# The last two expert blocks' rows stay in SBUF and are added to their tokens by one-hot products

## The chip, the cores and the metric

The kernel runs on one core of one Trainium2 chip. The metric is the device time of one execution in microseconds (us). Engines are named as the profile names them: PE is TensorE (matrix products, PEld its weight loads), DVE is VectorE, ACT is ScalarE, POOL is GpSimd, SP is SyncE, which here only issues DMAs. A q behind a name (POOLq, SPq) is that engine's instruction queue.

## The reference

One decoder layer over 512 tokens of 1024 features. What matters here is its last part, a mixture of 64 experts with 8 experts per token, and the layer norm that ends the program:

```
def routed_experts(xf, idx, gate_w, w_gate, w_up, w_down):
    # sort the token-expert assignments by expert, one or more blocks of rows per expert
    ...
    def block_fn(args):
        toks, e = args
        xb = x_pad[toks]
        return swiglu(xb, w_gate[e], w_up[e], w_down[e])
    yb = lax.map(block_fn, (row_tok.reshape(n_blocks, MOE_BLOCK), block_e))
    y = yb.reshape(n_rows, d) * row_w[:, None]
    return jax.ops.segment_sum(y, row_tok, num_segments=n_tok + 1)[:n_tok]
...
        moe = swiglu(xf, w_sh_gate[l], w_sh_up[l], w_sh_down[l]) + \
            routed_experts(xf, idx, gate_w, ...)
        x = layer_norm(ALPHA * x + moe.reshape(bsz, seq, d), ln3_g[l], ln3_b[l])
    return x
```

Each token's output is ALPHA times its input, plus the shared expert, plus the weighted rows of its eight experts, normalised over the 1024 features.

## The kernel before

Before the experts come the input projections, the two mixers, cross-attention, routing and the shared expert. None of that is touched. The expert stage runs N = 65 blocks in the order of the list `queue`: one block of up to 128 token rows for each of the 64 experts, and one overflow block (the entry None) for an expert with more than 128 rows. Blocks are numbered here from 0 to 64.

Every fp32 operand of a product is split into a high and a low fp32r part: `split` (L80) casts the high part on ACT and subtracts it on DVE for the low part. `mm3` (L83 to L85) then runs three products for one. Iteration n of the loop does, in source order, the up and gate products of block n (`block_up`, tiles ehi, elo), the gated hidden rows of block n - 1 (`block_h`, tiles hh, hth, htl), the loads of the weights of block n + 1 (`load_gu`, on SP), the split of the down weights of block n - 1 (`down_split`, tiles dhi, dlo), the token rows of block n + 1 (`prepare_x`: transposes, tile xb, and a gather on POOL), and the down products of block n - 1 (`block_down`). Weights land in ten SBUF slots that the class `Ring` hands out in turn; each block takes three of them.

`block_down` copies its two 128x512 PSUM results to the tile ys on ACT (L754, L755). A DMA from POOL (L756) then scatters the 128 rows to their tokens and adds them to a sum in DRAM. There are two such sums, `accs[0]` and `accs[1]` (acc_79 and acc_80 below, `accv` a view of each in four chunks of 128 tokens). They start as ALPHA times the input and as the shared expert. Blocks alternate between them by `target(n)`: block 61 goes to sum 0, block 62 to sum 1, and the last two blocks, 63 and 64, both to sum 0. A scatter waits for the one before it on the same sum.

In the last iteration the four chunks X[0] to X[3] (tiles y, two chunks each) are loaded by SP from sum 1 (L945). After the last block comes a loop over further overflow blocks (`tc.For_i`, L953) whose count is read from a register. With these inputs its body runs no time, but where it ends every engine waits until all engines and all DMAs issued so far are done. Behind it POOL adds sum 0 to X by four accumulating DMAs (L969). Each chunk is then normalised: chunks 0 and 2 by `centred` on DVE, chunks 1 and 3 by `norm_in` on ACT. The reciprocal square root is a power on POOL (L120, L152), DVE applies gain and shift (L979), and ACT issues the write of the output (L980).

Instructions stand on their engines in an order that a scheduler makes at build time; it may move an instruction ahead of the source's order, but not past what it depends on.

Of the kernel before, what the change touches and what calls it, by code (L numbers as in the profile page):

```python
# [9 lines left out]
FT = mybir.dt.float32  # L10
FR = mybir.dt.float32r
# [3 lines left out]
OP = mybir.AluOpType  # L15
# [3 lines left out]
T = 512  # L19
D = 1024  # L20
KC = 8
NCH = 4
# [5 lines left out]
ALPHA = 2.0 ** 0.25  # L28
# [10 lines left out]
def decoder_layer(ctx: ExitStack, tc: tile.TileContext, I, out, dbg=None):  # L39
    nc = tc.nc  # L40
# [41 lines left out]
    def mm3(ps, s, m, start, stop):  # L82
        nc.tensor.matmul(ps, s[0], m[0], start=start, stop=False)  # L83
        nc.tensor.matmul(ps, s[0], m[1], start=False, stop=False)  # L84
        nc.tensor.matmul(ps, s[1], m[0], start=False, stop=stop)  # L85
# [26 lines left out]
    def centred(dst, src, g):  # L112
        st = sm.tile([128, 2, 6], FT, name="st", tag="st")
        for j in range(2):
            nc.vector.bn_stats(st[:, j], src[:, j * 512:(j + 1) * 512])
        mv = sm.tile([128, 2], FT, name="mv", tag="mv")
        nc.vector.bn_aggr(mv, st)
        rs = sm.tile([128, 1], FT, name="rs", tag="rs")
        nc.vector.tensor_scalar(rs, mv[:, 1:2], EPS, None, op0=OP.add)
        nc.gpsimd.tensor_tensor(rs, rs, mhalf, op=OP.pow)  # L120
        nc.vector.scalar_tensor_tensor(dst, src, mv[:, 0:1], g, op0=OP.subtract, op1=OP.mult)
        return rs
# [6 lines left out]
    xTl = xp.tile([128, KC, T], FR, name="xTl", tag="xTl")  # L129
    X = row_pair("X01", "x01") + row_pair("X23", "x23")  # L130

    def residual(c, n0, ps, sums):
        sl = X[c][:, n0:n0 + 512]
        nc.vector.scalar_tensor_tensor(sl, sl, ALPHA, ps, op0=OP.mult, op1=OP.add,
                                       accum_out=sums[:, c, n0 // 512:n0 // 512 + 1])

    def norm_in(c, gb, junk):
        nm = sm.tile([128, 1], FT, name="nm", tag="nm")
        nc.scalar.activation(junk, X[c], AF.Identity, accum_out=nm)
        nc.vector.tensor_scalar(nm, nm, -1.0 / D, None, op0=OP.mult)  # L140
        return norm_tail(c, nm, gb, junk)
# [239 lines left out]
    with tc.tile_pool(name="pm", bufs=1, reuse_waits="tile") as pm:  # L381
# [34 lines left out]
        for c in range(NCH):  # L416
            cs = slice(c * 128, (c + 1) * 128)
            ps = accps()
# [305 lines left out]
    def block_h(hp, gate):  # L724
        hh = late[0].tile([128, EH], FT, name="hh", tag="hh")
        nc.scalar.activation(hh, hp[:, 0:EH], AF.Silu)
        mark[0] = nc.vector.scalar_tensor_tensor(hh, hp[:, EH:2 * EH], gate, hh, op0=OP.mult, op1=OP.mult)
        hv = hh.rearrange("t (p k) -> t k p", k=2)
        hps = zps().rearrange("p (k t) -> p k t", k=4)
        for k in range(2):  # L730
            nc.tensor.transpose(hps[:, k], hv[:, k], idf)
        hth = late[0].tile([128, 2, 128], FR, name="hth", tag="hth")
        htl = late[0].tile([128, 2, 128], FR, name="htl", tag="htl")
        split(hth, htl, hps[:, 0:2])
        return hth, htl

    def down_split(wd):
        w = []
        for k in range(2):
            hi = wq.tile([128, D], FR, name="dhi", tag="h")  # L740
            lo = wq.tile([128, D], FR, name="dlo", tag="l")
            split(hi, lo, wd[:, k])
            w.append((hi, lo))
        return w

    def block_down(w, h, idx, acc):

        yps = [accps(), accps()]
        for k in range(2):
            for j in range(2):  # L750
                js = slice(j * 512, (j + 1) * 512)
                mm3(yps[j], (h[0][:, k], h[1][:, k]), (w[k][0][:, js], w[k][1][:, js]), k == 0, k == 1)
        ys = late[0].tile([128, D], FT, name="ys", tag="ys")
        nc.scalar.copy(ys[:, 0:512], yps[0])  # L754
        nc.scalar.copy(ys[:, 512:1024], yps[1])  # L755
        nc.gpsimd.indirect_dma_start(out=accs[acc], out_offset=bass.IndirectOffsetOnAxis(ap=idx, axis=0),  # L756
                                     in_=ys, in_offset=None, bounds_check=T - 1, oob_is_err=False,
                                     compute_op=OP.add)
# [151 lines left out]
        block_x(gx.pop(queue[n]), n % 2)  # L910
        fetch_next()

    def target(n):
        return (n + 1) % 2 if n < N - 2 else 0

    ovx = []
    vs = block_views(0)
# [3 lines left out]
    for n in range(N):  # L921
        if n == N - 6:
            ring.drop(XT)
        idx, gt = entry(queue[n])
        hp = accps()
        block_up(gu, n % 2, 0, hp)
        if prev:
            h = block_h(prev[1], prev[3])
        block_up(gu, n % 2, 1, hp)
        down_v = vs[2]  # L930
        if n + 1 < N:
            vs = block_views(n + 1)
            gu = load_gu(*vs[0:2])
        if prev:
            wd = down_split(prev[0])
        if n + 1 < N:
            prepare_x(n + 1)
        if prev:
            block_down(wd, h, prev[2], target(n - 1))
        prev = (load_d(down_v), hp, idx, gt)  # L940
        if n == N - 1:

            X[:] = row_pair("y01", "x01") + row_pair("y23", "x23")
            for c in range(NCH):
                nc.sync.dma_start(X[c], accv[1][:, c])  # L945
            fg, fb = row_pair("fin", "t01")
            junk = xx.tile([128, D], FT, name="junk", tag="t2")
            nc.scalar.dma_start(fg, bcast(I["ln3_g"], D))
            nc.scalar.dma_start(fb, bcast(I["ln3_b"], D))
    block_down(down_split(prev[0]), block_h(prev[1], prev[3]), prev[2], 0)  # L950

    nov = nc.values_load(novi[0:1, 0:1], min_val=1, max_val=32)
    with tc.For_i(1, nov, 1):  # L953
        eii, *ov = overflow_list(opl)
        overflow_entry(*ov)
        idx, gt = entry(None)
        xg = gather(idx)
        vs = overflow_views(eii)
        gu, wd = load_gu(*vs[0:2]), load_d(vs[2])
        block_x(xg, 0)  # L960
        hp = accps()
        block_up(gu, 0, 0, hp)
        block_up(gu, 0, 1, hp)
        block_down(down_split(wd), block_h(hp, gt), idx, 0)


    ov_ = out[0].rearrange("(c t) d -> t c d", t=128)
    for c in range(NCH):
        nc.gpsimd.dma_start(X[c], accv[0][:, c], accum_op=OP.add)  # L969
    for c in range(NCH):  # L970
        if c in (0, 2):
            rs = centred(X[c], X[c], fg)
        else:
            rs = norm_in(c, (fg, None), junk)
        parts = 2 if c == NCH - 1 else 1
        w = D // parts
        for i in range(parts):
            sl = slice(i * w, (i + 1) * w)
            nc.vector.scalar_tensor_tensor(X[c][:, sl], X[c][:, sl], rs, fb[:, sl], op0=OP.mult, op1=OP.add)  # L979
            nc.scalar.dma_start(ov_[:, c, sl], X[c][:, sl])  # L980


class Ring:
# [10 lines left out]
    def drop(self, tags):  # L994
        self.slots = [s for s in self.slots if s[1] not in tags]

    def tile(self, shape):
        pool, tag = self.slots.pop(0)
        self.slots.append((pool, tag))
        return pool.tile(shape, FT, name="wraw", tag=tag, bufs=1)  # L1000


_INS = ["x", "mem", "ln_in_g", "ln_in_b", "w_in", "b_in", "ln_v_g", "ln_v_b", "w_spatial", "b_spatial",
# [22 lines left out]
```

## Time and profile before

| what | us |
|---|---|
| median of 3 runs | 1244.97 (1244.26 to 1245.07) |
| the profiled execution's own time | 1245.57 |
| its span, from first to last instruction | 1243.9 |
| PE busy in the span | 1180.3 (95%) |
| scatter of block 62 issued | 1196.47 |
| last copy of the last block out of PSUM begins | 1208.08 |
| last scatter landed, all engines released from the loop's end | 1218.29 |
| last chunk of the sum landed in X | 1232.82 |

The profile is one execution. Its page gives busy time by engine, the span in 40 slices, DMA queues, the chain of work that ended last, and the costliest groups of instructions. The trace behind it can be asked for the same by window, engine and line. The profiled execution's time is 1.67 us over its span, and the median of the runs is 0.60 us below that execution's time, so the median is the span and 1.07 us.

### The profile page before, as it was taken

What the parts mean: (1) busy time and instruction counts of PE and PEld (TensorE: products, weight loads), DVE (VectorE), ACT (ScalarE), POOL (GpSimd) and SP (SyncE); (2) the same over time, 40 slices, a digit from 0 to 9 for tenths busy, and PEclk for the clock granted to TensorE, in tenths of its full rate; (3) what the DMA queues carried; (4) which work ended last, traced back from release to release, by engine and by line L of the source; (5) the groups of instructions that cost most, each with busy time, mean ns of one, the idle gap of its engine ahead of it and who ended that gap; (6) DMA issues with size and microseconds to landing.
All of it is one profiled execution on the core that took longest, in us unless ns stands there. A gap on an engine that the chain in (4) does not pass through costs nothing.

```text
span 1243.9 us, 17778 instructions
## 1 busy us (share of the span) xinstructions
PE 1180.3 (95%) x6301; PEld 996.3 (80%) x6301; DVE 976.0 (78%) x1512; ACT 805.4 (65%) x1198; POOL 281.3 (23%) x179
## 2 busy tenths in 40 slices
PE   7999999999999999999999999999999999899980
PEld 6887888878888889887888888888888888788860
DVE  6546556464754577886999999999999999999974
ACT  6443334342324346536898888989889899699961
POOL 2000000000200010220334433434334343234313
PEclk9999999999999999999999999999999999899995
DMA  9621322224333223478999999999999999799946
GB/s 338 212 83 58 106 68 68 68 68 153 124 115 131 78 83 120 160 253 317 346 394 367 376 404 359 374 377 395 381 378 393 346 385 395 264 373 342 384 110 149
DMA packets 102368, 307.74 MB, mean 247 GB/s; under 512 B 17358, under 2 KB 35334, under 8 KB 93446
## 3 DMA queue, kind: packets, MB, share of 16 engines
q1 hardware_dynamic: 78054, 259.05, 54.6%
q0 software_dynamic: 19296, 35.71, 12.2%
q10 hardware_dynamic: 4928, 11.83, 2.5%
q8 instruction: 50, 0.82, 0.3%
q14 instruction: 40, 0.33, 0.1%
HBM read 298.64 MB, written 42.47 MB: 274 GB/s over the span
## 4 chain that ended last, share of the span: by engine, by line
PE 69%; DVE 9%; DMA 9%; issue 8%; POOL 3%; ACT 2%; SPq 0%; POOLq 0%; DVEq 0%; ACTq 0%
PE acc L84 20%; PE acc L85 20%; PE acc L83 20%; PE trp L170 4%; DMA wraw<-in_w_exp_gate_dram 2%; DMA acc<-ys,idxs 2%; DVE qq L283 2%; POOL acc L756 2%; DMA wraw<-in_w_exp_up_dram 1%; DMA wraw<-in_w_exp_down_dram 1%; DVE elo L80 1%; DMA ln<-in_ln_in_g_dram 1%; PE zp L84 1%; POOL xg L686 1%; PE zp L83 1%
## 5 line engine op out<-in xcount | busy, mean ns | idle before, releaser
L80 DVE TENSOR_TENSOR elo<-wraw,ehi 128x1024 fp32r<-128x1024 f32 x260 | 313.6, 1224 | 15.4 <-ACT ehi L80 14.4
L80 ACT CAST ehi<-wraw 128x1024 fp32r<-128x1024 f32 x260 | 274.3, 1056 | 45.5 <-PE acc L85 42.4
L84 PE MATMUL acc<-elo,xb 128*128 128x512 f32 x520 | 206.5, 397 | 5.1 <-DVE elo L80 3.9
L83 PE MATMUL acc<-ehi,xb 128*128 128x512 f32 x520 | 209.4, 403 | 1.2 <-ACT xb L80 1.2
L85 PE MATMUL acc<-ehi,xb 128*128 128x512 f32 x520 | 206.0, 396 | 1.1 <-DVE xb L80 1.1
L756 POOL DMA_INDIRECT acc<-ys,idxs x65 | 148.4, 2283 | 213.8 <-ACT ys L755 199.4
L80 DVE TENSOR_TENSOR wlo<-wraw,whi 128x1024 fp32r<-128x1024 f32 x84 | 101.9, 1223 | 105.1 <-ACT whi L80 105.1
L80 ACT CAST whi<-wraw 128x1024 fp32r<-128x1024 f32 x84 | 87.5, 1051 | 127.6 <-PE acc L84 72.1
L84 PE MATMUL acc<-xTl,whi 128*128 128x512 f32 (+1 forms) x448 | 162.3, 363 | 0.0
L83 PE MATMUL acc<-xTh,whi 128*128 128x512 f32 (+1 forms) x448 | 162.0, 362 | 0.0
L85 PE MATMUL acc<-xTh,wlo 128*128 128x512 f32 (+1 forms) x448 | 160.7, 360 | 0.0
L80 DVE TENSOR_TENSOR dlo<-wraw,dhi 128x1024 fp32r<-128x1024 f32 x130 | 156.6, 1220 | 0.4 <-ACT dhi L80 0.2
L80 ACT CAST dhi<-wraw 128x1024 fp32r<-128x1024 f32 x130 | 137.5, 1057 | 29.5 <-PE acc L85 21.4
L686 POOL DMA_INDIRECT xg<-x2d,idxs x65 | 90.3, 1389 | 231.0 <-PE trp L170 172.8
L84 PEld LDWEIGHTS acc<-elo,xb 128*128 128x128 f32 x520 | 98.4, 189 | 24.4 <-DVE elo L80 4.4
L85 PEld LDWEIGHTS acc<-ehi,xb 128*128 128x128 f32 x520 | 98.2, 189 | 22.0 <-DVE xb L80 2.0
L83 PEld LDWEIGHTS acc<-ehi,xb 128*128 128x128 f32 x520 | 98.8, 190 | 20.4 <-ACT xb L80 1.4
L83 PE MATMUL acc<-dhi,hth 128*128 128x512 f32 x260 | 106.1, 410 | 0.5 <-ACT hth L80 0.5
L85 PE MATMUL acc<-dhi,htl 128*128 128x512 f32 x260 | 102.9, 396 | 0.0
L84 PE MATMUL acc<-dlo,hth 128*128 128x512 f32 x260 | 102.5, 394 | 0.0
L83 PEld LDWEIGHTS acc<-xTh,whi 128*128 128x128 f32 x448 | 84.5, 189 | 12.1
L84 PEld LDWEIGHTS acc<-xTl,whi 128*128 128x128 f32 x448 | 84.6, 189 | 11.6
(278 smaller groups left out, 2168.8 us busy)
## 6 DMA issues: line engine op xcount, KB each, us to landing
wraw<-in_w_exp_gate_dram SPq DMA_DIRECT2D x130, 512.0 KB
wraw<-in_w_exp_up_dram SPq DMA_DIRECT2D x130, 512.0 KB
wraw<-in_w_exp_down_dram SPq DMA_DIRECT2D x65, 1024.0 KB
wraw<-in_w_in_dram SPq DMA_DIRECT2D x28, 1024.0 KB
wraw<-in_w_mem_kv_dram SPq DMA_DIRECT2D x4, 1024.0 KB
wraw<-in_w_out_dram SPq DMA_DIRECT2D x4, 1024.0 KB
X<-in_x_dram SPq DMA_DIRECT2D x4, 512.0 KB
wraw<-in_w_mem_q_dram SPq DMA_DIRECT2D x2, 1024.0 KB
```

The lines of the kernel that those rows point to most:

```text
L80: return nc.scalar.copy(hi, src), nc.vector.tensor_sub(lo, src, hi.bitcast(FT))
L83: nc.tensor.matmul(ps, s[0], m[0], start=start, stop=False)
L84: nc.tensor.matmul(ps, s[0], m[1], start=False, stop=False)
L85: nc.tensor.matmul(ps, s[1], m[0], start=False, stop=stop)
L170: nc.tensor.transpose(ps[:, k], sv[:, k0 + k], idf)
L283: nc.vector.tensor_tensor_scan(qq[:, 0:n][:, ::-1], sy[:, 1:n + 1][:, ::-1], ones.to_broadcast([128, n]), 1.0, op0=OP.mult, op1=OP.mult)
L686: nc.gpsimd.indirect_dma_start(out=xg, out_offset=None, in_=x2d, in_offset=bass.IndirectOffsetOnAxis(ap=idx, axis=0), bounds_check=T - 1, ...
L756: nc.gpsimd.indirect_dma_start(out=accs[acc], out_offset=bass.IndirectOffsetOnAxis(ap=idx, axis=0), in_=ys, in_offset=None, bounds_check=T ...
```

## The change

Block 63 and block 64 are no longer scattered. `block_keep` leaves the 128 rows of a block in SBUF, split into a high and a low part, in two ring slots, and makes a one-hot matrix oh[row, token] from the block's token numbers against the constant row 0 to 511 (iotaT). Behind the loop `kept_rows` forms, for each chunk of 128 tokens and each half of the features, the product of the one-hot matrix with those rows: four products (two blocks, high and low) into one PSUM tile, 32 in all. `residual` (L134, with scale 1) adds them to X on DVE and sums each row on the way. All four chunks are then normalised by `residual_norm`, with ACT's squares. SP loads X from sum 0 as it stands after block 61, and POOL adds sum 1, as it stands after block 62, by the four accumulating DMAs, which now stand ahead of the loop's end. The loop's own body, which doesn't run here, adds its rows in the same way.

```
-    def residual(c, n0, ps, sums):
+    def residual(c, n0, ps, sums, scale=ALPHA):
...
+    def block_keep(yps, idx):
+        tok = sm.tile([128, 1], FT, name="tok", tag="nm")
+        nc.vector.tensor_copy(tok, idx)
+        if not ohs:
+            o = ring.tile([128, 4, T], FR)
+            ohs.extend(o[:, i] for i in range(4))
+        oh = ohs.pop(0)
+        y = ring.tile([128, 2, D], FR)
+        hi, lo = y[:, 0], y[:, 1]
+        nc.vector.tensor_scalar(oh, iotaT, tok, None, op0=OP.is_equal)
+        for j in range(2):
+            js = slice(j * 512, (j + 1) * 512)
+            split(hi[:, js], lo[:, js], yps[j])
+        return oh, hi, lo
+
+    def kept_rows(kept, c, n0):
+        ps = accps()
+        last = 2 * len(kept) - 1
+        i = 0
+        for oh, hi, lo in kept:
+            for y in (hi, lo):
+                nc.tensor.matmul(ps, oh[:, c * 128:(c + 1) * 128], y[:, n0:n0 + 512], start=i == 0, stop=i == last)
+                i += 1
+        return ps
...
-    def target(n):
-        return (n + 1) % 2 if n < N - 2 else 0
+    kept, ohs = [], []
+    iotaT = xx.tile([128, T], FT, name="iotaT", tag="t3")
+    nc.gpsimd.iota(iotaT, pattern=[[1, T]], base=0, channel_multiplier=0, ...)
...
-        if prev:
-            block_down(wd, h, prev[2], target(n - 1))
+        if n == N - 1:
+            kept.append(block_keep(down(wd, h), prev[2]))
+        elif prev:
+            block_down(wd, h, prev[2], n % 2)
...
-                nc.sync.dma_start(X[c], accv[1][:, c])
+                nc.sync.dma_start(X[c], accv[n % 2][:, c])
...
+            for c in range(NCH):
+                nc.gpsimd.dma_start(X[c], accv[(n - 1) % 2][:, c], accum_op=OP.add)
-    block_down(down_split(prev[0]), block_h(prev[1], prev[3]), prev[2], 0)
+    kept.append(block_keep(down(down_split(prev[0]), block_h(prev[1], prev[3])), prev[2]))
...
+    sums = sm.tile([128, NCH, 2], FT, name="fsums", tag="fsums", bufs=1)
     for c in range(NCH):
-        nc.gpsimd.dma_start(X[c], accv[0][:, c], accum_op=OP.add)
-    for c in range(NCH):
-        if c in (0, 2):
-            rs = centred(X[c], X[c], fg)
-        else:
-            rs = norm_in(c, (fg, None), junk)
+        for n0 in (0, 512):
+            residual(c, n0, kept_rows(kept, c, n0), sums, 1.0)
+        rs = residual_norm(c, sums, (fg, None), junk)
```

On POOL, from the scatter of block 62 on, before (acc_79 is sum 0, acc_80 sum 1, the y tiles are X, xg and the last acc_79 row belong to the body of the loop that doesn't run):

```order
L756 DMA acc_80<-ys,idxs 512x1024
L756 DMA acc_79<-ys,idxs 512x1024 x2
L952 TENSOR_LOAD novi
L953 COMPARE_AND_BRANCH
...
L686 DMA xg_4790<-x2d,idxs 128x1024
L756 DMA acc_79<-ys,idxs 512x1024
...
L969 DMA y_12375<-acc_79 128x1024 x2
L969 DMA y_12376<-acc_79 128x1024 x2
```

and after, at the same place:

```order
L787 DMA acc_80<-ys,idxs 512x1024
L985 DMA y_12380<-acc_80 128x1024 x2
L985 DMA y_12381<-acc_80 128x1024 x2
L988 TENSOR_LOAD novi
L989 COMPARE_AND_BRANCH
...
L686 DMA xg_4790<-x2d,idxs 128x1024
L989 REGISTER_ALU
```

The two scatters to sum 0 are gone, and the four accumulating DMAs have moved from behind the loop's end to right behind the scatter of block 62.

On DVE, the end of the last block up to the read of the loop's count, before:

```order
L80 TENSOR_TENSOR dlo<-wraw,dhi 128x1024 x2
L727 SCALAR_TENSOR_TENSOR hh<-acc,gates,hh 128x256
L80 TENSOR_TENSOR htl<-zp,hth 128x256
L952 TENSOR_LOAD novi
L953 COMPARE_AND_BRANCH
```

and after:

```order
L727 SCALAR_TENSOR_TENSOR hh<-acc,gates,hh 128x256
L80 TENSOR_TENSOR wraw<-acc,wraw 128x512 x2
L80 TENSOR_TENSOR htl<-zp,hth 128x256
L80 TENSOR_TENSOR wraw<-acc,wraw 128x512 x2
L988 TENSOR_LOAD novi
```

The low parts of block 63's rows stand ahead of the htl of block 64, and those of block 64 behind it. The two one-hot matrices (L764) stand among the rows of blocks 62 and 63, each between two splits of up weights.

On DVE behind the loop's end, before (chunk 0 by BN_STATS, then chunk 1 by the squares from ACT):

```order
L115 BN_STATS st<-y_12375 128x6 x2
L117 BN_AGGR mv<-st 128x2
L119 TENSOR_SCALAR rs<-mv 128x1
L121 SCALAR_TENSOR_TENSOR y_12375<-y_12375,mv,fin 128x1024
L140 TENSOR_SCALAR nm<-nm 128x1
L979 SCALAR_TENSOR_TENSOR y_12375<-y_12375,rs,fin 128x1024
L151 TENSOR_SCALAR sq<-sq 128x1
L153 SCALAR_TENSOR_TENSOR y_12375<-y_12375,nm,fin 128x1024
```

and after (L134 adds the kept rows, L153 and L1017 apply gain and shift):

```order
L134 SCALAR_TENSOR_TENSOR y_12380,fsums<-y_12380,acc 128x512 x2
L145 TENSOR_SCALAR nm<-fsums 128x1
L134 SCALAR_TENSOR_TENSOR y_12380,fsums<-y_12380,acc 128x512 x2
L151 TENSOR_SCALAR sq<-sq 128x1
L153 SCALAR_TENSOR_TENSOR y_12380<-y_12380,nm,fin 128x1024
L145 TENSOR_SCALAR nm<-fsums 128x1
L1017 SCALAR_TENSOR_TENSOR y_12380<-y_12380,sq,fin 128x1024
L134 SCALAR_TENSOR_TENSOR y_12381,fsums<-y_12381,acc 128x512
L151 TENSOR_SCALAR sq<-sq 128x1
L153 SCALAR_TENSOR_TENSOR y_12380<-y_12380,nm,fin 128x1024
L134 SCALAR_TENSOR_TENSOR y_12381,fsums<-y_12381,acc 128x512
L1017 SCALAR_TENSOR_TENSOR y_12380<-y_12380,sq,fin 128x1024
```

Each chunk now has two 128x512 additions from PSUM and two passes over 1024 columns, with the additions of chunks 2 and 3 set between the passes of chunks 0 and 1. The last rows, not shown, are the second passes of chunk 2 and of chunk 3, the latter in two halves.

## Rows read from the trace of the kernel before

**Rows 1.** The page: busy tenths of TensorE in 40 slices of the span.

```profile
PE   7999999999999999999999999999999999899980
```

**Rows 2.** The chain that ended last, 1204 to 1222: start us, us, what.

```profile
1204.86 6.91 DMA acc<-ys,idxs
...
1212.51 5.78 DMA acc<-ys,idxs
...
1219.09 0.62 issue
```

**Rows 3.** Timeline from 1195 on: start, us, engine, line, operation; idle before in brackets.

```profile
1196.47 1.88 POOL L756 DMA_INDIRECT acc<-ys,idxs  x1 [7.52 <-ACT ys L755]
...
1201.97 1.76 SPq L945 DMA_DIRECT2D y<-acc  x4
...
1208.08 0.58 ACT L755 COPY ys<-acc 128x512 f32<-128x512 f32 x1
...
1219.71 3.63 POOL L969 DMA_DIRECT2D y<-acc  x4 [5.65 <-issue]
...
1232.82 1.06 ACT L139 ACTIVATE junk<-y 128x1024 f32<-128x1024 f32 x1 [2.38 <-DMA y<-acc]
...
1239.27 1.41 DVE L979 SCALAR_TENSOR_TENSOR y<-y,sq,fin 128x512 f32<-128x512 f32 x2 [0.44 <-POOL sq L152]
```

**Rows 4.** Line 953, the loop's end: its waits on TensorE's and VectorE's queues.

```profile
L953 DVEq EVENT_SEMAPHORE  x13: 21/50/7808, 1205.8 to 1219.0; - x13
L953 PEldq EVENT_SEMAPHORE  x13: 51/51/5672, 1208.1 to 1219.2; - x13
```

**Rows 5.** Windows: engines' busy us, then granted clock, DMA share, GB/s.

```profile
1203.00:1209.00 6.00, 4.50 (x19) 2.95 (x17) 1.41 (x3) 2.71 (x5) 1.56 (x1) 1.00 0.95 343
1212.00:1215.00 3.00, 0.00 (x0) 0.00 (x0) 0.00 (x0) 0.00 (x0) 1.56 (x1) 0.51 0.33 25
1221.00:1227.00 6.00, 0.00 (x0) 0.00 (x0) 1.92 (x5) 0.00 (x0) 2.53 (x4) 0.50 0.97 173
```

**Rows 6.** Timeline, POOL: the longest scatter seen, and one beside idle engines.

```profile
1149.52 4.93 POOL L756 DMA_INDIRECT acc<-ys,idxs  x1 [1.76 <-ACT ys L755]
...
1212.51 1.56 POOL L756 DMA_INDIRECT acc<-ys,idxs  x1 [6.09 <-DMA acc<-ys,idxs]
```

**Rows 7.** Timeline, TensorE, 1070 to 1077: 128x512 products after an idle stretch.

```profile
1071.07 0.80 PE L84 MATMUL acc<-elo,xb 128*128 128x512 f32 x1 [2.44 <-DVE elo L80]
...
1072.09 0.63 PE L83 MATMUL acc<-ehi,xb 128*128 128x512 f32 x1
1072.52 0.63 PE L84 MATMUL acc<-elo,xb 128*128 128x512 f32 x1
...
1076.47 0.40 PE L85 MATMUL acc<-ehi,xb 128*128 128x512 f32 x1
1076.71 0.40 PE L83 MATMUL acc<-ehi,xb 128*128 128x512 f32 x1
```

**Rows 8.** Timeline, 517 to 523 and 1229 to 1231: the steps of one chunk's norm.

```profile
517.74 1.28 DVE L153 SCALAR_TENSOR_TENSOR X<-X,nm,ln 128x1024 f32<-128x1024 f32 x1
518.93 0.68 DVE L134 SCALAR_TENSOR_TENSOR X<-X,acc 128x512 f32<-128x512 f32 x1
...
519.54 1.28 DVE L156 SCALAR_TENSOR_TENSOR X<-X,sq,ln 128x1024 f32<-128x1024 f32 x1
...
1229.19 1.15 ACT L150 ACTIVATE junk<-y,nm 128x1024 f32<-128x1024 f32 x1 [0.22 <-DVE nm L140]
...
1230.71 1.53 POOL L152 TENSOR_TENSOR sq<-sq,mhalf 128x1 f32<-128x1 f32 x1 [2.35 <-DVE sq L151]
```

**Rows 9.** VectorE's groups by shape, and one split of a late block in its timeline.

```profile
L779 DVE TENSOR_TENSOR oh<-iota,posm 128x512 bf16<-128x512 f32 x64 | 41.7, 687 | 0.0
...
1178.38 1.23 DVE L80 TENSOR_TENSOR elo<-wraw,ehi 128x1024 fp32r<-128x1024 f32 x1 [0.26 <-ACT ehi L80]
```

More of the change, by code (lines that the diff above doesn't have):

```diff
@@ L130, in decoder_layer @@
     X = row_pair("X01", "x01") + row_pair("X23", "x23")
-    def residual(c, n0, ps, sums):
+    def residual(c, n0, ps, sums, scale=ALPHA):
         sl = X[c][:, n0:n0 + 512]
-        nc.vector.scalar_tensor_tensor(sl, sl, ALPHA, ps, op0=OP.mult, op1=OP.add,
+        nc.vector.scalar_tensor_tensor(sl, sl, scale, ps, op0=OP.mult, op1=OP.add,
                                        accum_out=sums[:, c, n0 // 512:n0 // 512 + 1])
@@ L744, in down_split, with down @@
         return w
-    def block_down(w, h, idx, acc):
+    def down(w, h):
         yps = [accps(), accps()]
@@ L752, in block_down @@
                 mm3(yps[j], (h[0][:, k], h[1][:, k]), (w[k][0][:, js], w[k][1][:, js]), k == 0, k == 1)
+        return yps
+    def block_keep(yps, idx):
[21 more added lines that the diff above has]
+        return ps
+    def block_down(w, h, idx, acc):
+        yps = down(w, h)
         ys = late[0].tile([128, D], FT, name="ys", tag="ys")
@@ L911, in prepare_x @@
         fetch_next()
-    def target(n):
-        return (n + 1) % 2 if n < N - 2 else 0
+    kept, ohs = [], []
+    iotaT = xx.tile([128, T], FT, name="iotaT", tag="t3")
+    nc.gpsimd.iota(iotaT, pattern=[[1, T]], base=0, channel_multiplier=0, allow_small_or_imprecise_dtypes=True)
     ovx = []
@@ L963, in decoder_layer @@
         block_up(gu, 0, 1, hp)
-        block_down(down_split(wd), block_h(hp, gt), idx, 0)
+        more = [block_keep(down(down_split(wd), block_h(hp, gt)), idx)]
+        for c in range(NCH):
+            for n0 in (0, 512):
+                sl = X[c][:, n0:n0 + 512]
+                nc.vector.tensor_tensor(sl, sl, kept_rows(more, c, n0), op=OP.add)
     ov_ = out[0].rearrange("(c t) d -> t c d", t=128)
+    sums = sm.tile([128, NCH, 2], FT, name="fsums", tag="fsums", bufs=1)
     for c in range(NCH):
-        nc.gpsimd.dma_start(X[c], accv[0][:, c], accum_op=OP.add)
-    for c in range(NCH):
-        if c in (0, 2):
-            rs = centred(X[c], X[c], fg)
-        else:
-            rs = norm_in(c, (fg, None), junk)
+        for n0 in (0, 512):
+            residual(c, n0, kept_rows(kept, c, n0), sums, 1.0)
+        rs = residual_norm(c, sums, (fg, None), junk)
         parts = 2 if c == NCH - 1 else 1
@@ L995, in drop, with tile @@
         self.slots = [s for s in self.slots if s[1] not in tags]
-    def tile(self, shape):
+    def tile(self, shape, dtype=FT):
         pool, tag = self.slots.pop(0)
         self.slots.append((pool, tag))
-        return pool.tile(shape, FT, name="wraw", tag=tag, bufs=1)
+        return pool.tile(shape, dtype, name="wraw", tag=tag, bufs=1)
 _INS = ["x", "mem", "ln_in_g", "ln_in_b", "w_in", "b_in", "ln_v_g", "ln_v_b", "w_spatial", "b_spatial",
```

## Prediction

> **What bounds the kernel now.** I read the page's slices first: TensorE is at nine tenths or more from the second slice on and falls off only in the last two [rows 1]. So the expert loop is TensorE's, and what the change can touch is the stretch after its last products, some 36 us of 1243.9. Next the chain that ended last: it runs over POOL and DMAs alone. The scatter of block 63 takes 6.91 us from issue to landing, the scatter of block 64 waits for it and takes 5.78, and only then, at 1218.29, does anything else move [rows 2]. The timeline shows that the last block's copy out of PSUM began at 1208.08, so the results lay ready ten microseconds earlier [rows 3]. Line 953 shows why nobody ran ahead: TensorE's and VectorE's queues stood in semaphore waits of 5.7 and 7.8 us there and passed the last one at 1219 [rows 4]; the end of the loop waits for all DMAs. Behind it POOL issues the four accumulating DMAs at 1219.71, the last chunk lands at 1232.82, and the last VectorE instruction ends at 1239.27 + 1.41 = 1240.68, which is 3.2 us ahead of the span's end [rows 3]. From release to end: 1243.9 - 1218.29 = 25.6 us.
>
> **Part by part.**
>
> *The two scatters go.* That takes the waits of 6.91 and 5.78 us off the chain [rows 2]. What is late next is not the last block (ready about 1209) but the four accumulating DMAs, which now stand ahead of the loop's end. All engines wait there for all DMAs [rows 4], so the release comes when X is complete, and the time must be built from there.
>
> *Block 62's scatter.* It is issued at 1196.47, as before, since nothing ahead of it moves. In the trace SP's load, which waits for it, starts at 1201.97, 5.5 us later; the scatter that ran beside SP's four loads took 6.91 [rows 2, 3]. The loads of sum 0 now start when block 61's scatter has landed, one block (9.4 us) earlier, at about 1192.6. Before, they began 2.9 us ahead of a scatter, now 3.9, and they keep the DMA engines at 0.95 for 6 us [rows 5], so they are nearly through when the rows of this scatter move. I take 5.8, between the two ends and nearer to the undisturbed one: landed at 1202.3.
>
> *The reload.* POOL needed 0.62 us from its last wait to the first issue [rows 2], and 1232.82 - 1219.71 = 13.1 us from there to the last landing [rows 3]. The DMA engines were at 0.97 and moved only 173 GB/s in that stretch [rows 5], so it is the transfer that takes the time, and nothing else moves data then in either kernel. POOL's own share may be slower beside a busy VectorE: a scatter's issue took 1.88 us there and 1.56 beside idle engines [rows 3, 6]. I add 0.2 (ends: nothing, or 3.4 for the one issue of 4.93). Release: 1202.3 + 0.6 + 13.1 + 0.2 = **1216.2**, 2.1 us earlier than 1218.29.
>
> The Trainium skill speaks for more here. DMA: Bandwidth & Descriptors, section "Anatomy of one DMA", fits a DMA issued by GpSimd as 2.0 us and its bytes over 436 GB/s; by that the four would take an estimated 2.0 + 4.8 = 6.8 us and the sum would be 6.3 us lower. The trace disagrees with 13.1 us for accumulating ones, and I go by the trace; the rule gets no chance of its own.
>
> *What hides under that wait.* The last block's rows must now be split on VectorE (four subtractions of some 0.69 us by the nearest shape, two of them ahead of block 64's htl), and the one-hot matrices made, two of 0.69 us, during blocks 62 and 63 [rows 9]. ScalarE's four casts replace four copies of the same shape. Late blocks leave VectorE idle for 0.26 us and a little more [rows 9], so a one-hot pushes it by up to 0.4 us in a block whose rate TensorE sets; cost zero, or 1.4 us if VectorE were the bound. The splits end near 1209 + 1.4 = 1210.5, under the release by 5.7 us; without that cover they would cost 1.4 us. The two kept blocks take three more ring slots, so block 64's down weights go to a slot whose data is last read by the split at 1178.38 [rows 9]: 20 us before they are needed, cost zero. SP's loads stand behind that one and wait for 1192.6 anyway. The constant iotaT is one POOL instruction long before the experts: zero.
>
> *From release to the first product.* Before, POOL took 1219.71 - 1218.29 = 1.4 us over the remaining waits and its issue [rows 3]. TensorE now does the same and starts products: 1.5, so 1217.7.
>
> *The tail.* TensorE has then been idle for nine microseconds. Three microseconds of idleness were enough before: the granted clock was 1.00 in 1203 to 1209 and 0.51 in 1212 to 1215 [rows 5], the level of 1.2 GHz. Products of this shape start every 0.43 us at that level and every 0.24 at the full one; after the stop that ended at 1071.07 they ran slow past 1072.52 and were fast by 1076.47 [rows 7]. I take 4.5 us of slow ones. A chunk's half is four products, so the first ten or so products are slow and the fourth half is summed 6.0 us after the first product starts (3.9 at full clock, 7.0 if it stayed low). From there VectorE is the bound. Its rows start 1.19 us apart for a pass of 1024 columns and 0.61 for an addition of 512 from PSUM (517.74, 518.93, 519.54) [rows 8]. What is left then is five additions (3.1), seven passes (8.3), two halves (1.4) and small steps (0.7): 13.5. The second pass of chunk 0 must also wait for its square on ScalarE (1.15) and the power on POOL (1.53) [rows 8], which by the order of the rows leaves 0.7 us of holes: 14.2. The end after it is 3.2 as before, and 0.3 more because the last two chunks' writes now follow closely. Sum: 6.0 + 14.2 + 3.5 = 23.7, so the tail with its 1.5 us is 25.2, against 25.6 before. The additions cost what the parallel landing and norming gave back.
>
> **Sum.** 1217.7 + 23.7 = 1241.4 of span, 2.5 us less than 1243.9. The median stands 1.07 us over the span, so 1244.97 - 2.5 = **1242.5 us**. A measurement of this kernel can tell about 0.2%, 2.5 us, from no change, so the forecast lies on that border.
>
> **Rivals.**
>
> 1. *The loop's end does not hold the engines for the reload.* TensorE and VectorE would start at 1210.5 + 1.5 = 1212.0 and find chunk 0 landed or nearly so: 1212.0 + 23.7 = 1235.7, time 1236.8. Against it speak the long waits of all queues there [rows 4].
>
> 2. *The gain is eaten at the restart.* Before, VectorE had its first data 6 us after the release; now TensorE and VectorE need instructions at once, behind a jump. No row prices a fetch of code; POOL, which did go on at once, needed 0.62 us [rows 2]. I bound it by zero and by the 3.2 us from the last VectorE instruction to the end, a round trip to DRAM included. With TensorE at the low level throughout (1.0 more) this makes up to 4.2: 1243.5 to 1246.7, say 1245.0: no change. The Trainium skill, Runtime: NRT & Kernel Launch, section "Instruction fetch mechanics", says that a taken branch to a page that isn't loaded stalls until it is fetched; no run here shows that yet.
>
> 3. *POOL can't write the descriptors while VectorE is busy: slower.* The reload moves from an idle machine to the last block's splits. If the first of its DMAs got out only when VectorE is done, at 1210.5, the last would land at 1223.6 and the end be 1223.6 + 25.2 = 1248.8, time 1249.9. It decides once the issue is held to 1207.9, five microseconds late, where the time is 2.5 us over the median. For it stands the issue of 4.93 us, against it 1.88 in the same stage [rows 3, 6] and gaps in VectorE's last microseconds (1.41 us busy of 6) [rows 5]. The Trainium skill, SBUF — State Buffer, section "SBUF: two separate sides", has such a lock for some VectorE modes; the 1.88 us beside the busy loop show little of it.
>
> **Chances.** The forecast's mechanism has 0.70: half of it faster by over 0.2%, half within. Rival 1 has 0.05, rival 2 has 0.17, rival 3 has 0.08. That makes faster 0.41, same 0.51, slower 0.08. The range: downwards the full clock at once (2.1) with a scatter of 5.5 us and no slower issue (0.5) give 1239.9, a little more room makes 1239.5; upwards a scatter of 6.9 (1.1), the low clock (1.0) and part of a fetch (1.5) give 1246.0. Rivals 1 and 3 lie outside, 0.13 in all.
>
> **What would show it.** In the changed profile: SP's load at 1192 to 1193; POOL's four accumulating issues at about 1203 and no scatter after block 62's; waits at the loop's end on all queues until about 1216, and the first of 32 products 1.5 us later at 0.5 of the clock; VectorE without idle stretches over half a microsecond from 1224 on; last VectorE instruction near 1238. The sum is wrong if the release comes before 1215 or after 1218, or if VectorE waits for TensorE beyond chunk 1. The expert loop's blocks must still be 9.4 us apart; if those of blocks 62 and 63 are longer, the one-hots were not hidden.

## The result: slower by one per cent

| | before | after |
|---|---|---|
| median, us (lowest to highest) | 1244.68 (1243.05 to 1246.84), 6 runs | 1257.76 (1253.55 to 1261.21), 6 runs |
| ratio to before, 95% interval | | 1.0097 (1.0086 to 1.0107) |
| profiled execution, time and span | 1245.57, 1243.9 | 1261.21, 1259.5 |
| block 62's scatter issued | 1196.47 [rows 3] | 1211.42 |
| from there to the end of the span | 47.4 | 48.1 |

The forecast was 1242.5, within 1239.5 to 1246.0. The last two lines of the table say where to look. What the change touches, the stretch behind block 62's scatter, costs nearly what it cost before. The 15 us went earlier, in a stretch that the diff does not touch. (The profiled execution of after is the slowest of its six, so its spans are a little long: 1259.5 against 1251.8 to 1256.1 of the others. By the medians the loss is 13 us.)

The page of after, TensorE's slices; only the last slice differs from [rows 1]:

```profile
PE   7999999999999999999999999999999999899983
```

The chain that ended last, after: start us, us, what.

```profile
1211.42 6.19 DMA acc<-ys,idxs
...
1218.25 0.72 POOL y L985
...
1220.15 13.48 DMA y<-acc
1233.63 1.48 issue
1235.11 5.06 PE acc L777 x11
```

This is the path that the prediction named, step for step: the scatter of block 62 (6.19 us), 0.64 us to POOL's first issue, the four accumulating DMAs until 1233.63 (15.4 us from the first issue), 1.48 us over the loop's end, and the first product by a one-hot. It stands 15 us late. POOL's rows show how the delay is spread; timeline of POOL, before and then after: start, us, engine, line, operation.

```profile
1187.07 1.88 POOL L756 DMA_INDIRECT acc<-ys,idxs  x1 [7.52 <-ACT ys L755]
```

```profile
1201.89 2.12 POOL L787 DMA_INDIRECT acc<-ys,idxs  x1 [7.52 <-ACT ys L786]
1211.42 1.88 POOL L787 DMA_INDIRECT acc<-ys,idxs  x1 [7.41 <-ACT ys L786]
```

Before, these blocks are 9.40 us apart (1187.07, and 1196.47 in [rows 3]); after, 9.53. From the scatter of block 0 (594.27 before, 602.37 after) to that of block 62 the loss is 6.9 us in all. But the experts had started late already; first weight load of an expert's product (PEld), before and after:

```profile
573.81 0.19 PEld L83 LDWEIGHTS acc<-ehi,xb 128*128 128x128 f32 x1 [1.41 <-ACT xb L80]
```

```profile
580.18 0.19 PEld L83 LDWEIGHTS acc<-ehi,xb 128*128 128x128 f32 x1 [1.41 <-ACT xb L80]
```

So 6.4 us are lost ahead of the experts, in stages whose code did not change. The 1.7 us that are left of the 14.95 fall into block 0, where the granted clock of this one execution was 0.72 in 580 to 586 (before, 1.00 in 573.6 to 579.6). Weight loads in the input projections, before and after: each product has one, so their starts give the pace.

```profile
317.82 0.19 PEld L84 LDWEIGHTS acc<-xTl,whi 128*128 128x128 f32 x1
...
320.31 0.19 PEld L83 LDWEIGHTS acc<-xTh,whi 128*128 128x128 f32 x1
```

```profile
318.05 0.19 PEld L85 LDWEIGHTS acc<-xTh,wlo 128*128 128x128 f32 x1
...
320.61 0.19 PEld L84 LDWEIGHTS acc<-xTl,whi 128*128 128x128 f32 x1
```

In each pair the second row is the eleventh start after the first: 2.49 / 11 = 226.4 ns a product before, 2.56 / 11 = 232.7 after. TensorE is busy without a gap there in both, and the granted clock is the same; windows of TensorE, before and after (busy us, instructions, granted clock, DMA share, GB/s):

```profile
300.00:420.00 120.00, 120.00 (x566) 1.00 0.34 116
```

```profile
300.00:420.00 120.00, 120.00 (x553) 1.00 0.36 119
```

So TensorE does not wait here, the clock does not fall, and still each 128x512 product takes 6 ns longer. TensorE's busy share does not show it, 120 of 120 us in both; that of its weight loads does, which are spread thinner (100.25 us before, 97.76 after in these windows). About 1,344 such products stand ahead of the experts (the groups xTh with whi and wlo, whi and wlo with xTh, with Mh), which at 6 ns makes 8.1 us, a little more than the 6.4 that reach the experts.

### The profile page after: what moved, and what is told of

It is laid out like the page before. It is cut to its first block, busy times and chain, and to the rows that moved or that the text cites. A ratio compares the mean times of both kernels' runs of the same rounds, so it can differ in the third digit from the quotient of the medians.

```text
span 1259.5 us, 17863 instructions
## 1 busy us (share of the span) xinstructions
PE 1206.2 (96%) x6333; PEld 1004.7 (80%) x6333; DVE 982.9 (78%) x1532; ACT 805.4 (64%) x1198; POOL 256.9 (20%) x178
## 4 chain that ended last, share of the span: by engine, by line
PE 71%; DVE 10%; issue 8%; DMA 5%; POOL 3%; ACT 2%; SPq 0%; DVEq 0%; POOLq 0%; ACTq 0%
PE acc L84 21%; PE acc L85 21%; PE acc L83 21%; PE trp L170 3%; DVE qq L283 2%; DMA acc<-ys,idxs 1%; POOL acc L787 1%; DVE elo L80 1%; DVE oh L810 1%; DMA wraw<-in_w_exp_gate_dram 1%; DMA y<-acc 1%; DMA ln<-in_ln_in_g_dram 1%; PE zp L84 1%; PE zp L85 1%; POOL xg L686 1%
## 5 line engine op out<-in xcount | busy, mean ns | idle before, releaser
L83 PE MATMUL acc<-ehi,xb 128*128 128x512 f32 x520 | 212.8, 409 | 1.2 <-ACT xb L80 1.2
L85 PE MATMUL acc<-ehi,xb 128*128 128x512 f32 x520 | 208.0, 400 | 1.2 <-DVE xb L80 1.2
L80 DVE TENSOR_TENSOR wlo<-wraw,whi 128x1024 fp32r<-128x1024 f32 x84 | 101.9, 1221 | 109.5 <-ACT whi L80 109.3
L787 POOL DMA_INDIRECT acc<-ys,idxs x63 | 129.7, 2059 | 209.9 <-ACT ys L786 207.5
L686 POOL DMA_INDIRECT xg<-x2d,idxs x65 | 84.2, 1296 | 253.3 <-PE trp L170 197.2
L84 PEld LDWEIGHTS acc<-xTl,whi 128*128 128x128 f32 x448 | 84.5, 189 | 13.3
```

The costliest lines, as they stand in the source:

```text
L80: return nc.scalar.copy(hi, src), nc.vector.tensor_sub(lo, src, hi.bitcast(FT))
L686: nc.gpsimd.indirect_dma_start(out=xg, out_offset=None, in_=x2d, in_offset=bass.IndirectOffsetOnAxis(ap=idx, axis=0), bounds_check=T - 1, ...
```

## What was suspected

The final norm needs a new small tile, `sums` (named fsums), of 32 bytes a partition. It is taken from the pool sm, which lies below almost everything that is allocated later. By the addresses of the two built programs the raw weights move from 56800 to 56832, xTh from 122336 to 122368 and xb from 138720 to 138752, and most tiles allocated later with them, each by 32 bytes; the weights' halves whi, wlo, ehi, elo, dhi, dlo lie below sm and stay (the first at 23008). Before, the two operands of the large products stood at the same place within 256 bytes: 23008, 122336 and 138720 all leave 224.

Theory A: this shift of 32 bytes between the two operands costs TensorE some nanoseconds a product. Rival B: something else of the change (instructions, their place in the code) does it. Below them, two local questions of the prediction: does the reload hold the loop's end, and can it be made shorter.

## Experiments: where the 15 us went

**The change without the shift.** The sums are put into a slot that exists already.

```
-    sums = sm.tile([128, NCH, 2], FT, name="fsums", tag="fsums", bufs=1)
+    sums = sm.tile([128, 2, 6], FT, name="fsums", tag="st").rearrange("p a b -> p (a b)")[:, 0:2 * NCH]...
```

> The changed kernel, with its two sums of the final norm put into an existing slot of 96 bytes instead of a new tile of 32, so that every tile of SBUF lies where it lay in the kernel before; nothing else differs. Theory A (the new tile of 32 bytes moves the operands of TensorE's products by 32 bytes, and each product takes some nanoseconds more): the scatter of block 62 is issued at 1196 to 1197 us instead of 1211.4, blocks are 9.40 us apart instead of 9.52, and the time is 1257.8 less the 15 us that the scatter was late, 1243, with 1241 to 1246 taken as a hit. Theory B (something else of the change does it: its instructions, their place in the code, the iota at the start, the moved work in the last blocks): the place of a tile does not matter, the time stays at 1256 to 1261 and the scatter at 1210 to 1212.

Measured: 1243.58 us, ratio to before 0.9987 (0.9978 to 0.9997). Chain that ended last: start us, us, what.

```profile
1196.26 5.81 DMA acc<-ys,idxs
...
1202.71 0.72 POOL y L985
...
1204.61 11.80 DMA y<-acc
1216.41 1.48 issue
1217.89 5.78 PE acc L777 x16
```

Block 62's scatter is back at 1196.26, and the change itself is worth 0.13%, which is within the 0.2% that the prediction calls no change. All that made it slower was the place of one tile.

**The shift without the change.** The kernel before gets an unused tile in sm of 32, 64 or 128 bytes a partition.

```
+    pad = sm.tile([128, 8], FT, name="pad", tag="pad", bufs=1)    # 16 and 32 in the other two
+    nc.vector.memset(pad, 0.0)
     ov_ = out[0].rearrange("(c t) d -> t c d", t=128)
```

> The kernel before, with one unused tile of 32 bytes per partition and one memset of it ahead of the last norm: its tiles lie as in the changed kernel, and none of the change is in it. Theory A: the loss of 15 us comes without the change, so 1244.7 + 15 = 1259.7, with 1256 to 1262 taken as a hit, and blocks 9.52 us apart. Theory B: 1244 to 1246, blocks 9.40 us apart.

> As the one with 32 bytes, with 64. Theory A says only that the place matters. If what counts is the place within 64 bytes, the tiles stand as before and the time is 1244 to 1246; if it is the place within 128 bytes, or how the two operands stand to each other in a longer period, the time differs, 1248 to 1262. Theory B: 1244 to 1246.

> As the one with 32 bytes, with 128. Theory A: where the period is 32 times some power of two up to 128 bytes, the time is back at 1244 to 1246; if it stays near 1259, the cause is not a period of up to 128 bytes but the move against the tiles that stand still, or the unused tile itself. Theory B: 1244 to 1246.

Measured: 1258.25 with 32 bytes (ratio 1.0120, 1.0094 to 1.0146), 1253.19 with 64 (1.0074, 1.0058 to 1.0091), 1256.13 with 128 (1.0087, 1.0070 to 1.0104). POOL in the timeline with 32 bytes, two late blocks:

```profile
1199.69 1.88 POOL L756 DMA_INDIRECT acc<-ys,idxs  x1 [7.64 <-ACT ys L755]
1209.22 1.88 POOL L756 DMA_INDIRECT acc<-ys,idxs  x1 [7.65 <-ACT ys L755]
```

An unused tile alone gives the whole loss, with blocks 9.53 apart; B falls. (One memset writes it; the kernel below in which nearly all tiles move has the same memset and no loss.) But the expected simple period falls too: 128 bytes do not bring the time back. What the place is counted against was still open.

**Which tiles, and place or distance.** In one kernel the 32 bytes lie between the raw weights and x's tiles (in the pool xx); in the other ahead of nearly all tiles (in the pool cp), the weights' halves included.

```
+    pad = xx.tile([128, 8], FT, name="pad", tag="pad")      # the first kernel
```

```
     mhalf = cp.tile([128, 1], FT, name="mhalf")
+    pad = cp.tile([128, 8], FT, name="pad")                 # the second kernel
```

> The kernel before with the unused 32 bytes between the raw weights and the tiles of x (xTh, xTl, xb, hth and the rest behind them): the raw weights, which the DMAs write and the splits read, stay where they lay, and only x's side moves against the weights' halves whi, wlo, ehi, elo. If the place of TensorE's own operands to each other is what costs (A): as with all of them moved, blocks 9.52 us apart and 1256 to 1262. If it is the place of the raw weights (D): 9.40 us and 1243 to 1247.

> The kernel before with the unused 32 bytes ahead of nearly all its tiles, the weights' halves whi, wlo, ehi, elo, dhi and dlo among them: nearly every tile of the left side moves by 32 bytes, and the stationary and the moving operands of the large products keep their distance. If the distance decides (A, as the 128 stretches have it: 226.7 ns a product at a distance of 0 or 256, 230 to 240 at nearly all others): 1243 to 1247 and blocks 9.40 us apart. If the place of a tile itself decides: 1256 to 1262 and 9.52 us.

Measured: 1255.83 with the raw weights left in place, but for the ring slots that lie among x's tiles (one run, beside 1244.99 for the kernel before), and 1244.13 with nearly all tiles moved (ratio 0.9990, 0.9980 to 0.9999). POOL in the two timelines:

```profile
1197.47 1.88 POOL L756 DMA_INDIRECT acc<-ys,idxs  x1 [7.65 <-ACT ys L755]
1206.99 1.88 POOL L756 DMA_INDIRECT acc<-ys,idxs  x1 [7.65 <-ACT ys L755]
```

```profile
1184.48 1.89 POOL L758 DMA_INDIRECT acc<-ys,idxs  x1 [7.47 <-ACT ys L757]
1193.84 1.89 POOL L758 DMA_INDIRECT acc<-ys,idxs  x1 [7.47 <-ACT ys L757]
```

9.52 apart in the first, 9.36 in the second. Moving the raw weights, which DMAs write and the splits read, is not needed for the loss. And moving everything together by the same 32 bytes costs nothing: the distance between the two operands counts, not where either lies.

**The products by themselves.** A kernel that runs only 128x128 by 128x512 products, sixteen stretches of 32, each with another pair of places; first alone (L74), then beside ScalarE's and VectorE's splits (L86), then beside DMAs (L96).

> None of the layer is computed: 96 products to start, and then three times the same sixteen stretches of 32 products of 128x128 by 128x512, in which the stationary tile stands 0, 32, 64 or 96 bytes behind a multiple of 128 and the moving one too. First with nothing beside them, then with ScalarE and VectorE splitting a tile of 128x1024 over and over, then with DMAs loading 2 MB pieces. If TensorE's own reads decide (A), the sixteen of the first stretch differ by some 6 ns a product, from 227 to 234. If it is a collision with the writes of others (C), the first sixteen are equal within 1 ns, at 213 to 228, and those of the second or third differ. If all are equal in each of the three, the place within 128 bytes is not what counts.

TensorE's groups by line: line, engine, operation, operands, count, busy us, mean ns.

```profile
L86 PE MATMUL acc<-m,s 128*128 128x512 f32 x512 | 118.6, 393 | 0.0
L96 PE MATMUL acc<-m,s 128*128 128x512 f32 x512 | 118.6, 393 | 0.0
L74 PE MATMUL acc<-m,s 128*128 128x512 f32 x512 | 118.5, 393 | 0.0
```

The three sets of 512 products take the same time to 0.1 us, so neither the splits (ScalarE and VectorE each busy for about half of the second set) nor the DMAs (411 GB/s in the third) have a part in it; a collision with others' writes falls. Within each set the sixteen pairs differ, by their starts from 226.7 to 234.2 ns a product, equal places (0 and 0, 32 and 32 and so on) at 226.7 to 227.1 in the first set. The sign counts as well: a moving operand 64 bytes ahead of the stationary one gave 229.3, one 64 behind it 233.1. With a period of 128 the two would be the same distance, so it had to be another.

**Every distance.** The same products, 128 stretches of 16 with nothing beside them; the moving operand starts 0, 4, 8 ... 508 bytes further on.

> None of the layer is computed: 96 products to start, and then 128 stretches of 16 products of 128x128 by 128x512 with nothing beside them, in which the moving tile stands 0, 4, 8 ... 508 bytes further on than the stationary one, counted from the same place within 512 bytes; each stretch has a line of its own. Theory A, as the sixteen pairs of the last such run bear it out (226.7 to 227.0 ns a product at 0, 229.3 at 64, 233.0 to 234.2 at 32, 96, 416, 448 and 480): the pitch is a function of this distance alone, lowest at 0, where the kernel before stands. Theory E: the seven distances seen are not the best ones, and some other gives less than 226, so that a kernel with its tiles put there would beat both.

TensorE's timeline: start, us, engine, line. L65 is distance 0, and each line 4 bytes more: L66 is 4, L73 32, L81 64, L97 128, L113 192, L129 256.

```profile
34.37 3.79 PE L65 MATMUL acc<-mv,st 128*128 128x512 f32 x16
37.99 3.95 PE L66 MATMUL acc<-mv,st 128*128 128x512 f32 x16
41.79 3.88 PE L67 MATMUL acc<-mv,st 128*128 128x512 f32 x16
...
64.16 3.89 PE L73 MATMUL acc<-mv,st 128*128 128x512 f32 x16
67.89 3.98 PE L74 MATMUL acc<-mv,st 128*128 128x512 f32 x16
...
94.02 3.83 PE L81 MATMUL acc<-mv,st 128*128 128x512 f32 x16
97.69 3.98 PE L82 MATMUL acc<-mv,st 128*128 128x512 f32 x16
...
154.00 3.88 PE L97 MATMUL acc<-mv,st 128*128 128x512 f32 x16
157.71 3.99 PE L98 MATMUL acc<-mv,st 128*128 128x512 f32 x16
...
213.86 3.89 PE L113 MATMUL acc<-mv,st 128*128 128x512 f32 x16
217.59 3.93 PE L114 MATMUL acc<-mv,st 128*128 128x512 f32 x16
...
273.75 3.79 PE L129 MATMUL acc<-mv,st 128*128 128x512 f32 x16
277.38 3.95 PE L130 MATMUL acc<-mv,st 128*128 128x512 f32 x16
```

From one line's start to the next, divided by 16: 226 ns at 0, 238 at 4, 233 at 32, 229 at 64, 232 at 128, 233 at 192, and 227 again at 256. By the starts of the weight loads, which the figures from here on go by, the pattern repeats with a period of 256 bytes (each of the distances from 256 on is within 0.3 ns of the one 256 lower), and 0 is the only good one: the next lowest are at 229.8, the highest, 88, at 239.9. Theory E, a better place than that of the kernel before, falls.

With this table the pads can be read. In most products of the projections (960 of the 1,344) x is the moving operand, in the others and in the experts' up products it is the stationary one, so a pad of 64 bytes is a distance of +64 (229.9) in the first and of 192 (233.1) in the second: that is why it cost less than the pads of 32 (233.2 at 32 and at 224) and 128 (232.4 in both). The trace of the kernel with 64 bytes bears it out. Weight loads in a projection with x moving, eleven starts apart:

```profile
317.84 0.19 PEld L85 LDWEIGHTS acc<-xTh,wlo 128*128 128x128 f32 x1
...
320.36 0.19 PEld L84 LDWEIGHTS acc<-xTl,whi 128*128 128x128 f32 x1
```

That is 229.1 ns a product, where the pad of 32 gave 232.7, while the late blocks are 9.53 us apart with either pad (scatters at 1194.34 and 1203.87 here). What stays open is why the distance counts. That the products and the weight loads of the next ones read SBUF at the same time would fit, but no run here separates the two reads. That a pad of 256 is harmless in the whole kernel is not shown either, for want of room in SBUF; only the products by themselves show that period.

## Experiments: what holds the loop's end

The next three have the tiles where they lay before, so they compare with the 1243.58 above.

**Without the reload of the second sum.**

```
-            for c in range(NCH):
-                nc.gpsimd.dma_start(X[c], accv[(n - 1) % 2][:, c], accum_op=OP.add)
```

> The changed kernel with its tiles where they lay before, without the four DMAs that add the second sum, which is so missing from the output. If these DMAs hold the loop's end (the prediction's step), the first product by a one-hot starts 1.5 us after the last kept row is split (1209.2), at 1210 to 1212 instead of 1217.9, and the time falls by 6 to 8 us, to 1236 to 1238. If something else holds it, the time stays at 1242 to 1245.

Measured: 1234.13 (one run). In the timeline, block 64's gated rows and the last split on VectorE, and TensorE behind the loop:

```profile
1203.71 0.48 DVE L727 SCALAR_TENSOR_TENSOR hh<-acc,gates,hh 128x256 f32<-128x256 f32 x1
...
1208.21 1.37 DVE L80 TENSOR_TENSOR wraw<-acc,wraw 128x512 fp32r<-128x512 f32 x2 [2.38 <-ACT wraw L80]
1210.39 7.55 PE L777 MATMUL acc<-wraw 128*128 128x512 f32 x32 [2.15 <-DVEq L987]
```

The products start at 1210.39 instead of 1217.89: the four DMAs do hold the loop's end, as the prediction had it. Of the 9.4 us that were won, 7.5 are this and 1.9 are TensorE's clock, which was not in what was expected: after a stop of 2.2 us it was still at 1.00, after one of ten at 0.50 (windows 1211 to 1214 of this kernel and 1218 to 1221 of the one with the reload: busy us, instructions, granted clock), and 32 products took 7.55 us instead of 9.39.

```profile
1211.00:1214.00 3.00, 3.00 (x15) 1.00 0.00 0
```

```profile
1218.00:1221.00 3.00, 3.00 (x7) 0.50 0.00 0
```

**Three blocks kept, the reload one block earlier.**

```
-        if n == N - 1:
+        if n >= N - 2:
             kept.append(block_keep(down(wd, h), prev[2]))
...
-        if n == N - 1:
+        if n == N - 2:
             X[:] = row_pair("y01", "x01") + row_pair("y23", "x23")
```

> The changed kernel with its tiles where they lay before, and three blocks kept instead of two: the reload starts behind block 61's scatter, one block of 9.4 us earlier, and 48 products stand behind the loop instead of 32. If the reload alone holds the loop's end, it is done by then: first product at 1210 to 1212, two more products ahead of the first residual (0.9 us), a time of 1236 to 1239 and a ratio to before of 0.992 to 0.995. If another wait takes its place (a ring slot that the third kept block takes from the weights to come, or the splits on ScalarE and VectorE), 1242 or more.

Measured: 1240.56, ratio to before 0.9960 (0.9946 to 0.9974): better than two blocks, less than expected. POOL, VectorE and TensorE in the timeline, and the waits of POOL's queue ahead of the reload (shortest, median and longest in ns):

```profile
1187.13 2.14 POOL L787 DMA_INDIRECT acc<-ys,idxs  x1 [7.37 <-ACT ys L786]
1196.82 3.63 POOL L985 DMA_DIRECT2D y<-acc  x4 [7.56 <-DVE wraw L80]
...
1205.34 0.47 DVE L727 SCALAR_TENSOR_TENSOR hh<-acc,gates,hh 128x256 f32<-128x256 f32 x1
...
1209.86 1.38 DVE L80 TENSOR_TENSOR wraw<-acc,wraw 128x512 fp32r<-128x512 f32 x2 [2.62 <-ACT wraw L80]
...
1212.04 12.76 PE L777 MATMUL acc<-wraw 128*128 128x512 f32 x48 [2.15 <-DVEq L989]
```

```profile
L985 POOLq EVENT_SEMAPHORE  x9: 17/43/9088, 1186.9 to 1198.2; - x9
```

The first product comes at 1212.04, the late end of what was expected, and two waits end there almost together. The reload started late: POOL's queue stood 9.1 us, until 1196.3, for the scatter of block 61 (issued at 1187.13; the VectorE split that the row names is only what ended last by the profile), and the reload's last landing is at 1210.41 in the trace. With the 1.48 us seen above it would have let the first product start at 1211.9. The last split of kept rows ends at 1211.24, 0.8 us ahead of the first product, as it does without the reload (1209.58 and 1210.39). The splits now stand ahead of block 64's gated rows (L727) on VectorE, which run at 1205.34 instead of 1203.71 in the kernel without the reload. So the splits hold the first product here, but by no more than some 0.15 us over the reload. The larger price is behind it: the 48 products take 12.76 us, until 1224.8, and VectorE waits for the last of them, so that from the first product to the end of the span it takes 26.5 us instead of the 23.9 with two blocks.

**The reload by plain DMAs.** SP loads the second sum into the tiles of gathered rows, and VectorE adds it.

```
-                nc.gpsimd.dma_start(X[c], accv[(n - 1) % 2][:, c], accum_op=OP.add)
+                nc.sync.dma_start(xgs[c], accv[(n - 1) % 2][:, c])
...
+    for c in range(NCH):
+        nc.vector.tensor_tensor(X[c], X[c], xgs[c], op=OP.add)
     nov = nc.values_load(novi[0:1, 0:1], min_val=1, max_val=32)
```

> The changed kernel with its tiles where they lay before; the second sum is loaded by four plain DMAs of SP's queue into the four free tiles of gathered rows and added by four additions of VectorE ahead of the loop's end, in place of the four accumulating DMAs of GpSimd's queue (14 to 15 us from the first issue to the last landing). If those DMAs are what the loop's end waits for: 2.1 MB at the 340 GB/s of the expert stage take 6.2 us and 2 us to start, so landed at 1210.6, the last addition done 1.2 us later, the first product at 1212.6 instead of 1217.9 and a time of 1237 to 1240, ratio to before 0.994 to 0.997. If the plain loads are no quicker than the accumulating ones (the rows' reads from DRAM behind the scatter limit both), or the additions hold the split of the last kept row: 1242 to 1245.

Measured: 1238.08, ratio to before 0.9943 (0.9929 to 0.9956), the best version of the study. SP, VectorE and TensorE in its timeline:

```profile
1200.90 1.74 SPq L985 DMA_DIRECT2D xg<-acc  x4
...
1208.21 2.47 DVE L989 TENSOR_TENSOR y<-y,xg 128x1024 f32<-128x1024 f32 x2 [0.20 <-DMA xg<-acc]
...
1211.18 10.36 PE L777 MATMUL acc<-wraw 128*128 128x512 f32 x32 [4.53 <-DVEq L991]
```

The last two additions start at 1208.21, when the third chunk has landed, and run on without a gap, so the fourth landed by 1209.4: 7.3 to 8.5 us from the first issue at 1200.90, where the accumulating DMAs needed 13.7 for the same sum (1202.71 to 1216.41 in the first experiment). The kind of DMA and the queue that issues it changed together, so which of the two makes it shorter is not shown. TensorE's clock gave part of the gain back: after a stop of 4.5 us it was at 0.50 in 1211 to 1214, and the 32 products took 10.36 us. The Trainium skill (DMA: Bandwidth & Descriptors, section "Anatomy of one DMA") has a fit for DMAs issued by GpSimd, by which the four take an estimated 6.8 us; the plain loads, issued by SP, come nearer to that figure than the accumulating ones that GpSimd issued.

## Why the prediction was wrong, and where it was right

- **The step that failed** is the first term of the sum: block 62's scatter "is issued at 1196.47, as before, since nothing ahead of it moves". Nothing ahead of it moved in the order of instructions; the operands moved in SBUF. The scatter came at 1211.42, 14.95 us late: a new tile of 32 bytes put the two operands of TensorE's large products at another distance, and each took some 6 ns longer (232.7 for 226.4 in the projections); only the 1.7 us of block 0 belong to a fallen clock. The prediction counted what the added tile does to the engines and not where it lies, and no rival covered it. Its own check, "the expert loop's blocks must still be 9.4 us apart", is the one that showed it (9.53), though it looked only for the one-hots there.
- **With the place put right, the sum holds.** Against the kernel without the shift: scatter issued 1196.26 (1196.47), 5.81 us to land (5.8), 0.64 to the first issue (0.6), 13.7 for the reload (13.3), 1.48 to the first product (1.5), which came at 1217.89 (1217.7), and 23.9 of tail (23.7): a span of 1241.8 (1241.4) and a time of 1243.58 (1242.5). Of the 1.1 us in the time 0.4 are the span; the rest is the step from span to median, taken at 1.07. The tail was sized right with its low clock: ten products in the first four microseconds (1218 to 1222, clock 0.52), the fourth half summed 6.5 us after the first product (6.0), then VectorE as the bound for 13.6 (14.2), and 3.8 to the end (3.5).
- **In the changed kernel itself** two terms were too small: the reload took 15.4 us instead of 13.3 and the scatter 6.19 instead of 5.8. Together with the tail (24.4) they ate the gain of 2.5 us that was forecast behind the scatter, and 0.7 more. Both are near their sizes above once the tiles are back, in one profiled execution each; what made them longer was not tested.
- **Rival 1** (the loop's end does not hold the engines for the reload) fell: without those DMAs the first product comes 7.5 us earlier, so with them it is held. **Rival 2** (the restart costs up to 4.2 us) fell: 1.48 us from the last landing to the first product, as before. **Rival 3** (POOL cannot write descriptors beside VectorE) fell: POOL's first issue came 0.64 us after the scatter landed and its four took 3.63 us, as they took 3.63 beside idle engines [rows 3].
- **The one-hots and splits** were hidden, as costed: in the kernel without the shift, with all of them in place, the blocks are 9.40 us apart again (scatters at 1186.86 and 1196.26). The price of 1.4 us that the prediction gives the last block's splits without the reload's cover was not measured by itself; with three blocks kept they hold the first product some 0.15 us longer than the reload would.
- **Two small slips in the sums** change nothing: the chances given add up to 0.40 for faster and 0.52 for same, not 0.41 and 0.51, and the upper end of the range to 1246.1.

## What to carry to other kernels

A tile has an address, and adding one, however small, moves all that its pool stack allocates after it. Ahead of any other reading of a change that adds or resizes SBUF tiles, compare the addresses of the operands of the hot products before and after, and compare the pace of back-to-back products in a stage that the change does not touch; TensorE's busy share does not show it. Put new small tiles into slots that exist, as was done here, or behind the large ones (which was not run), and if a sum must be reloaded at the end, plain loads with additions on an idle engine can be much shorter than accumulating DMAs, as they were here.

## What the hardware showed that was not expected

The pace of 128x512 fp32r products depends on the distance between the starts of the moving and the stationary operand: 226.7 ns at a multiple of 256 bytes, 229.8 to 239.9 at any other multiple of four, with nothing else running and the clock at its full level. The Trainium skill (SBUF — State Buffer, section "Who interferes with whom") gives TensorE two independent read ports for the moving operand and the weight load; here the pace depends on how the two operands lie to each other, and no run shows whether the ports are the cause. The Trainium skill (TensorE: Matmul & The Clock Gate, section "Back-to-back issue gap") gives a sustained 131 ns for a product of 512 columns in a stream of weight loads and products, and 512 / 2.4 + 2.5, an estimated 215.8 ns, for an isolated one. For the fp32r stream here the measurement stands against both: the fastest of all 128 distances was 226.7.

Four accumulating DMAs of 512 KB issued by GpSimd took 13.1 to 15.4 us from the first issue to the last landing in four kernels, and four plain loads issued by SP 7.3 to 8.5 in one.
